# An encoder layer in split single precision: low parts by GpSimd instead of accumulating DMAs, and a convolution that accumulates in PSUM

## The chip, the core and the metric

The kernel runs on one core of a Trainium2 chip. The metric is the device time of one execution in microseconds (us). Before the change it is 1473.66 us, the median of 3 runs (1470.12 to 1475.76). The core has a matrix engine (TensorE, PE in the profile; its weight loads are PEld), three engines for elementwise work (VectorE, DVE; ScalarE, ACT; GpSimd, POOL), a queue that issues DMAs (SyncE, SP), and 16 DMA engines. GpSimd has a DMA queue of its own. Each engine works through its own instructions in the order of the program.

## What is computed

One layer is applied to two groups of tokens with the same weights: the prompt (512 tokens) and the sample (1024 tokens), both of width 1024. Everything is float32. Cut to what matters, and without biases:

```python
h = rms_norm(x, g_pre) * (1 + scale) + shift          # scale, shift, gate from c
a_val, a_glu, a_z, u, v, b_z, g_a, g_b = split(h @ w_in)   # 8 blocks of 1024 columns
a = depthwise_conv(a_val * sigmoid(a_glu), conv_w)    # 31 taps along the tokens
y_a = (silu(layer_norm(a)) * silu(a_z)) @ conv_proj
v = layer_norm(gelu(v))
mixed = einsum("gpq,bnqgc->bnpgc", w_s, v)            # chunks of 128 tokens
y_b = (gelu(u) * mixed * silu(b_z)) @ sgu_proj
m = sigmoid(g_a) * y_a + sigmoid(g_b) * y_b
out = x + gate * rms_norm(m @ w_out, g_post)
```

## The kernel before

**Split operands.** A float32 matrix is multiplied as a high part and a low part. `hi` is the matrix rounded to a shorter type (a cast on ACT) and `lo = x - hi`. A product is three matmuls: hi·hi, hi·lo and lo·hi (lines 449 to 451 for a block of output columns, 472 to 474 for a block of output rows, 483 to 485 for the sample's products). Almost all matmuls have 128 rows of weights and 512 columns.

**Units.** A unit is one 128x1024 block of weights (512 KB). SP loads it into a `raw` tile, ACT casts it to `hi` (line 247), and then the low part is made in one of two ways. With `by_dma`, ACT writes the rounded `-raw` into `lo` (line 250) and GpSimd's queue issues a DMA that adds `raw` to it (line 240), which leaves `raw - hi`. Without it, DVE subtracts (line 259). `raw`, `hi` and `lo` are rings of four tiles each, so a later load waits for the low part of an earlier unit.

**Order.** A planner in Python runs four clocks (PE, DVE, ACT and the plan of loads) while it writes the program. The list `steps` holds what PE does: a step of 24 matmuls is planned at 5.25 us (`PLAIN`), a product of 12 matmuls at half of that (`PROD`). Between the steps the planner puts the work that belongs to a step (`a1`, `d1`, `a2`, `d2`) and fills DVE's clock up with background generators (`bg`): the convolutions (`conv_gen`), the layer norms (`ln_gen`), the preparation of the sample's operands (`prep1` to `prep3`), and so on. So the order on every engine is fixed when the program is built.

**The stages on PE.** A head of some 45 us (modulation and the first seven column blocks in quarters). Then the prompt: the GLU columns (steps up to 16), the `v` columns (`steps_v`), `u`, `b_z` with the mixing products (`mix_mm`), the gates, the projections and `steps_o`. Then the `v` columns of the sample's halves `sa` and `sb`. Then 28 **pairs**: a pair takes two blocks of 128 columns and both halves of the sample through 7 products instead of 8. For this it needs sums and differences of the two weight blocks (`T12`, `T34`, lines 1056 to 1063, on DVE), which are split too: `a` is the block itself (DVE subtracts, line 1079), `b`, `c` and `d` are made by `neg` on ACT (line 1068) and the accumulating DMA. The pairs come in groups: 8 for the GLU, then gB, um (`u` times the mixed `v`), hB (times silu of `b_z`), z, gA, four pairs each. Last come the projections of the halves (`post_B`, `post_A`) and their outputs (`steps_o`).

**Results of a pair.** ACT snapshots the bank X or Z after a product (`snap`, line 1014), because the next product adds to the same bank. DVE then adds (`d_c11`, `d_c22`, `d_c12`, lines 1018 to 1026), ACT applies a function (lines 1126, 1148, 1167), and in um and hB DVE multiplies four times (line 1158). PSUM's eight banks form one ring of eight (`bank()`).

**The convolution.** 31 scalar_tensor_tensor instructions per channel block (line 403), two blocks in turn, each on 512 tokens (prompt) or 1024 (sample). The accumulator is in SBUF: in the slot `S` for the prompt, in `c` for the sample. The sample's results go to DRAM and come back for the layer norm (`late_ln`), whose two means are matmuls with a constant (`bcast_mean`, lines 331 and 332); in the program these stand in the steps of `post_B` and later.

## Time and profile before

The profiled execution took 1466.83 us; its trace spans 1464.9 us. The other runs took 1470.12 to 1475.76 us.

| | busy us | share of the span |
|---|---|---|
| PE | 1432.5 | 98% |
| DVE | 1129.0 | 77% |
| ACT | 742.3 | 51% |
| POOL | 186.2 | 13% |

The page's rows on DMA say that 229.85 MB go through SP's queue and 90.72 MB through GpSimd's; the chain of work that ended last is PE for 80% and DMA for 11%. A busy PE is not PE at its peak, since matmuls are pipelined and their ends are modelled; what is counted below is how many matmuls a stretch holds. In a row of the windows view the columns are the stretch, its length, then PE, PEld, DVE, ACT and POOL, each with busy us and (x instructions), then the granted TensorE clock, the busy share of the DMA engines, and GB/s.

### The profile page before, as it was taken

The page shows a single profiled execution, that of the slowest core. Times are in us where ns is not written, and L with a number is a line of the kernel's source. Part 1 is how long each engine was busy: PE and PEld are TensorE (multiplying, and loading weights), DVE is VectorE, ACT ScalarE, POOL GpSimd, SP SyncE. Part 2 cuts the span into 40 slices and gives each one's busy share as a digit, 9 for nine tenths or more (in the row PEclk, how much of TensorE's full clock was granted, in tenths as well). Part 3 has the DMA queues.
Part 4 walks back from the last instruction along what each step waited for, and adds up shares of the span by engine and source line. Part 5 has one row for each costly group of instructions (what it writes and reads, how often), then busy time and mean ns, then how long its engine had stood idle before and what let it go on. Part 6 is the DMA issues. An engine that isn't in the chain of part 4 may idle for free.

```text
span 1464.9 us, 17769 instructions
## 1 busy us (share of the span) xinstructions
PE 1432.5 (98%) x6332; PEld 1169.3 (80%) x6332; DVE 1129.0 (77%) x1596; ACT 742.3 (51%) x1064; POOL 186.2 (13%) x220
## 2 busy tenths in 40 slices
PE   8999999999999989999999999999999989999997
PEld 4688888888888878888888888877888867888886
DVE  6769999976356455867999898898999939587645
ACT  3532544553486454454545565555556545554442
POOL 0000111111111110011111111111111100000000
PEclk9999999999999999999999999999999999999999
DMA  9266787897999998967666878877977799878782
GB/s 342 79 215 182 198 201 166 203 256 181 279 266 244 284 263 272 281 168 201 155 158 166 209 194 242 255 211 218 256 192 191 194 307 276 265 222 237 211 269 72
DMA packets 120040, 321.68 MB, mean 220 GB/s; under 512 B 13328, under 2 KB 17040, under 8 KB 119184
## 3 DMA queue, kind: packets, MB, share of 16 engines
q1 hardware_dynamic: 88992, 229.85, 45.2%
q0 software_dynamic: 30960, 90.72, 33.7%
q8 instruction: 49, 0.80, 0.2%
q14 instruction: 39, 0.32, 0.1%
HBM read 182.10 MB, written 47.71 MB: 157 GB/s over the span
## 4 chain that ended last, share of the span: by engine, by line
PE 80%; DMA 11%; DVE 4%; issue 2%; ACT 2%; SPq 1%; DVEq 0%; ACTq 0%; POOLq 0%
PE b L451 11%; PE b L449 11%; PE b L450 11%; PE b L483 10%; PE b L484 10%; PE b L485 10%; PE b L473 4%; PE b L474 4%; PE b L472 4%; DMA lo<-raw 2%; DMA wk<-d 2%; PE b L568 1%; DMA raw<-in_w_blk_dram 1%; DMA raw<-in_sproj_dram 1%; DVE c L403 1%
## 5 line engine op out<-in xcount | busy, mean ns | idle before, releaser
L483 PE MATMUL b<-A,hi 128*128 128x512 f32 x784 | 306.8, 391 | 6.9 <-ACT wk L1014 6.9
L484 PE MATMUL b<-A,hi 128*128 128x512 f32 x784 | 305.8, 390 | 0.0
L485 PE MATMUL b<-A,lo 128*128 128x512 f32 x784 | 305.7, 390 | 0.0
L449 PE MATMUL b<-A,hi 128*128 128x512 f32 x776 | 303.7, 391 | 0.0
L451 PE MATMUL b<-A,lo 128*128 128x512 f32 x776 | 302.8, 390 | 0.2 <-DMA lo<-raw 0.2
L450 PE MATMUL b<-A,hi 128*128 128x512 f32 x776 | 302.8, 390 | 0.0
L403 DVE SCALAR_TENSOR_TENSOR c<-c,prm 128x1024 f32<-128x1024 f32 x240 | 297.3, 1278 | 0.6
L247 ACT CAST hi<-raw 128x1024 fp32r<-128x1024 f32 x145 | 152.0, 1048 | 262.4 <-DMA raw<-in_w_v_dram 61.7
L240 POOL DMA_DIRECT2D lo<-raw x131 | 113.4, 865 | 788.8 <-ACT lo L250 690.8
L483 PEld LDWEIGHTS b<-A,hi 128*128 128x128 f32 x784 | 147.6, 188 | 40.1 <-ACT wk L1014 9.7
L485 PEld LDWEIGHTS b<-A,lo 128*128 128x128 f32 x784 | 147.6, 188 | 30.5
L484 PEld LDWEIGHTS b<-A,hi 128*128 128x128 f32 x784 | 147.5, 188 | 30.6 <-DVE A L967 0.2
L451 PEld LDWEIGHTS b<-A,lo 128*128 128x128 f32 x776 | 146.1, 188 | 31.3 <-DMA lo<-raw 0.7
L449 PEld LDWEIGHTS b<-A,hi 128*128 128x128 f32 x776 | 146.1, 188 | 30.4 <-issue 0.2
L450 PEld LDWEIGHTS b<-A,hi 128*128 128x128 f32 x776 | 146.0, 188 | 30.5 <-issue 0.2
L403 DVE SCALAR_TENSOR_TENSOR S<-c,prm,S 128x512 f32<-128x512 f32 x240 | 162.6, 745 | 0.2
L473 PE MATMUL b<-lo,A 128*128 128x512 f32 x384 | 150.6, 392 | 5.0 <-DMA lo<-raw 5.0
L472 PE MATMUL b<-hi,A 128*128 128x512 f32 x384 | 150.8, 393 | 0.0
L474 PE MATMUL b<-hi,A 128*128 128x512 f32 x384 | 150.0, 391 | 0.0
L240 POOL DMA_DIRECT2D lo<-T x84 | 72.4, 862 | 456.7 <-ACT lo L1068 374.0
L1014 ACT COPY wk<-b 128x512 f32<-128x512 f32 x112 | 65.0, 585 | 121.2 <-PE b L485 117.5
L250 ACT ACTIVATE lo<-raw 128x1024 fp32r<-128x1024 f32 x103 | 108.7, 1055 | 0.0
(206 smaller groups left out, 1630.7 us busy)
## 6 DMA issues: line engine op xcount, KB each, us to landing
raw<-in_w_blk_dram SPq DMA_DIRECT2D x105, 512.0 KB, 5.6
lo<-raw POOLq DMA_DIRECT2D x103, 512.0 KB, 6.6
d<-wk SPq DMA_DIRECT2D x142, 256.0 KB, 3.7
wk<-d SPq DMA_DIRECT2D x116, 256.0 KB, 5.9
lo<-T POOLq DMA_DIRECT2D x28, 512.0 KB, 5.7
lo<-T POOLq DMA_DIRECT2D x56, 256.0 KB, 4.4
raw<-in_w_v_dram SPq DMA_DIRECT2D x24, 512.0 KB, 5.6
raw<-in_sproj_dram SPq DMA_DIRECT2D x24, 512.0 KB, 6.1
```

The source lines that it names most:

```text
L240: GP.dma_start(lo.bitcast(F32), src, accum_op=ALU.add)
L247: S.copy(u.hi, u.raw)
L403: lambda: V.scalar_tensor_tensor(acc, in0=win, scalar=wt, in1=acc, op0=ALU.mult, op1=ALU.add))
L449: PE.matmul(dst, lhsT=wh3[:, k, :], rhs=hi, start=(k == 0), stop=False)
L450: PE.matmul(dst, lhsT=wh3[:, k, :], rhs=lo, start=False, stop=False)
L451: PE.matmul(dst, lhsT=wl3[:, k, :], rhs=hi, start=False, stop=(k == NK - 1))
L472: PE.matmul(banks[i], lhsT=hi, rhs=wh3[:, kk, :], start=(k == 0), stop=False)
L473: PE.matmul(banks[i], lhsT=hi, rhs=wl3[:, kk, :], start=False, stop=False)
L474: PE.matmul(banks[i], lhsT=lo, rhs=wh3[:, kk, :], start=False, stop=(k == NK - 1))
L483: PE.matmul(dst, lhsT=wh3[:, k, :], rhs=hi, start=st, stop=False, skip_group_check=True)
L484: PE.matmul(dst, lhsT=wh3[:, k, :], rhs=lo, start=False, stop=False, skip_group_check=True)
L485: PE.matmul(dst, lhsT=wl3[:, k, :], rhs=hi, start=False, stop=sp, skip_group_check=True)
```

## The change

1. **Low parts.** Every low part of a unit and of a pair is a subtraction on GpSimd (`rest`, line 249 of the new file): `by_dma`, the negated copy on ACT, the accumulating DMA and DVE's subtractions (lines 259 and 1079) are gone. The head's first seven blocks keep DVE's.
2. **Sums of weights.** `T12` and `T34` are made by GpSimd (`gsub`), ahead of the low parts in the same queue.
3. **PSUM.** The ring of eight banks becomes a ring of four banks (`ps`) and two double banks (`pd`). The convolution's accumulators are double banks; so are the banks of the means, of the sample's mixing, and of the second half of `steps_v` (sample) and `steps_o`. At the end of a channel block ACT copies the accumulator out.
4. **Order.** The group gB moves behind z. The two layer norms of the sample follow the convolution directly and are written to DRAM as `hA`; the operands of `post_A` are then made like those of `post_B` (`act_gen`). A third window tile lets a convolution's input be fetched earlier.

The diff, cut to its core:

```diff
-    ps = ctx.enter_context(tc.tile_pool(name="ps", bufs=8, space=bass.MemoryType.PSUM))
+    ps = ctx.enter_context(tc.tile_pool(name="ps", bufs=4, space=bass.MemoryType.PSUM))
+    pd = ctx.enter_context(tc.tile_pool(name="pd", bufs=2, space=bass.MemoryType.PSUM))
...
+    def double():
+        return pd.tile([P, 2 * T], F32, tag="b2", name="b2")
+    def four(more):
+        if not more:
+            return [bank() for _ in range(4)]
+        d = [double(), double()]
+        return [d[i // 2][:, (i % 2) * T:(i % 2) * T + T] for i in range(4)]
...
-    def lo_by_dma(lo, src):
-        GP.dma_start(lo.bitcast(F32), src, accum_op=ALU.add)
+    def rest(lo, x, hi):
+        GP.tensor_tensor(out=lo, in0=x, in1=hi.bitcast(F32), op=ALU.subtract)
...
             S.copy(u.hi, u.raw)
             clk["act"] += 0.96
-            if u.by_dma:
-                S.activation(u.lo, u.raw, AF.Copy, scale=-1.0)
-                clk["act"] += 0.96
-                lo_by_dma(u.lo, u.raw)
-                u.raw = True
-                live["raw"] -= 1
-    def unit_dve(u):
-        if not u.by_dma and u.raw is not True:
-            r, h, w = u.raw, u.hi, u.lo
-            dv(1.14, lambda: V.tensor_sub(w, r, h.bitcast(F32)))
+            rest(u.lo, u.raw, u.hi)
             u.raw = True
             live["raw"] -= 1
...
-            b = bank()
+            b = double()[:, 0:T]
             PE.matmul(b, lhsT=onemr, rhs=hi, start=True, stop=False)
...
-                ch.acc = accs(ch.j)
+                ch.acc = double()[:, 0:w]
...
-                        banks[:] = [bank() for _ in range(4)]
+                        banks[:] = four(h == 1 and t is not t0)
...
-        m = bank()
+        m = bank() if t is t0 else double()[:, 0:T]
...
+        def gsub(o, x, y):
+            GP.tensor_tensor(out=o, in0=x, in1=y, op=ALU.subtract)
         def t12():
-            dv(0.65, lambda: V.tensor_sub(half(t_, 1), half(u2.raw, 0), half(u1.raw, 0)))
-            dv(0.65, lambda: V.tensor_sub(half(t_, 0), half(u2.raw, 1), half(t_, 1)))
+            gsub(half(t_, 1), half(u2.raw, 0), half(u1.raw, 0))
+            gsub(half(t_, 0), half(u2.raw, 1), half(t_, 1))
...
+        def both(n, x):
+            hi, lo = part_tile("hi"), part_tile("lo")
+            w[n] = (hi, lo)
+            S.copy(hi, x)
+            rest(lo, x, hi)
+            clk["act"] += 0.96
         def act_b():
-            neg(lo, w["t12"])
-            lo_by_dma(lo, w["t12"])
-            S.copy(hi, w["t12"])
-            clk["act"] += 1.92
+            both("b", w["t12"])
...
         def out(j, acc):
             accd[j] = scratch(D)
-            put(accd[j], acc)
-            free[j % 2] = clk["dve"] + 4.0
+            for i in range(2):
+                x = wk()
+                ac(0.53, lambda: S.copy(x, acc[:, i * T:(i + 1) * T]))
+                put(accd[j][:, i * T:(i + 1) * T], x)
...
-        yield from late_ln(sa)
+        for t in halves:
+            yield from late_ln(t)
...
             dv(0.62, lambda: V.tensor_mul(z, z, t.acc[j]))
-            kept[j] = (z, ac(0.53, lambda: S.copy(t.hA.hi(j), z)))
+            spill("hA", t.half, j, z)
...
-    for name, b0, fin in (("gB", 56, lambda j: pair_func("gB", AF.Sigmoid, j)),
-                          ("um", 24, lambda j: pair_mul("um", AF.Gelu_apprx_tanh, "mx", j)),
+    for name, b0, fin in (("um", 24, lambda j: pair_mul("um", AF.Gelu_apprx_tanh, "mx", j)),
                           ("hB", 40, lambda j: pair_mul("hB", AF.Silu, "um", j)),
                           ("z", 16, lambda j: pair_func("z", AF.Silu, j)),
+                          ("gB", 56, lambda j: pair_func("gB", AF.Sigmoid, j)),
```

GpSimd's queue in the pairs, before. A row is one instruction: its line, its kind, the tile that it writes, the tiles that it reads, and the shape. The rows are those of one pair (`lo` of b, of c in two halves, of d) and the first two of the next:

```order
L240 DMA lo_7781<-T12_7741 128x1024
L240 DMA lo_7828<-T34_7786 128x512
L240 DMA lo_7828<-raw_7639 128x512
L240 DMA lo_7878<-T34_7786 128x512
L240 DMA lo_7944<-T12_7904 128x1024
L240 DMA lo_7991<-T34_7949 128x512
```

The same place in the changed kernel, one pair:

```order
L1054 TENSOR_TENSOR T12_7384<-raw_7289,raw_7287 128x512
L1054 TENSOR_TENSOR T12_7384<-raw_7289,T12_7384 128x512
L249 TENSOR_TENSOR lo_7388<-raw_7287,hi_7387 128x1024
L1054 TENSOR_TENSOR T34_7430<-raw_7289 128x512
L1054 TENSOR_TENSOR T34_7430<-raw_7287,T12_7384 128x512
L249 TENSOR_TENSOR lo_7434<-T12_7384,hi_7433 128x1024
L249 TENSOR_TENSOR lo_7487<-T34_7430,hi_7486 128x512
L249 TENSOR_TENSOR lo_7487<-raw_7289,hi_7486 128x512
L249 TENSOR_TENSOR lo_7535<-T34_7430,hi_7534 128x512
```

Four DMA issues per pair have become nine subtractions, two of 1024 columns and seven of 512, all with operands in SBUF.

DVE in a pair of the group hB, before: the sums, the low part of a, the additions (lines 1018, 1022, 1026) and multiplications (line 1158) of the results, and the convolution (line 403, accumulator in the tile `c8`) between them:

```order
L1018 TENSOR_TENSOR wk_7875<-b_7883,wk_7875 128x512
L1056 TENSOR_TENSOR T12_7904<-raw_7803,raw_7801 128x512
L1057 TENSOR_TENSOR T12_7904<-raw_7803,T12_7904 128x512
L1079 TENSOR_TENSOR lo_7900<-raw_7801,hi_7899 128x1024
L1158 TENSOR_TENSOR wk_7875<-wk_7875,wk_7896 128x512
L403 SCALAR_TENSOR_TENSOR c8_5283<-c8_5283,prm_83 128x1024 x2
L1062 TENSOR_TENSOR T34_7949<-raw_7803 128x512
L1063 TENSOR_TENSOR T34_7949<-raw_7801,T12_7904 128x512
L403 SCALAR_TENSOR_TENSOR c8_5283<-c8_5283,prm_83 128x1024
L1022 TENSOR_TENSOR wk_7973<-wk_7973,wk_7941 128x512
```

In the changed kernel, the first half of a pair of the same group (line 1019 was 1018, 1023 was 1022, 1151 was 1158, 402 was 403):

```order
L1019 TENSOR_TENSOR wk_7198<-b_7205,wk_7198 128x512
L402 SCALAR_TENSOR_TENSOR b2_6938<-c8_5158,prm_86,b2_6938 128x1024
L402 SCALAR_TENSOR_TENSOR b2_6582<-c8_5158,prm_86,b2_6582 128x1024
L1151 TENSOR_TENSOR wk_7198<-wk_7198,wk_7218 128x512
L402 SCALAR_TENSOR_TENSOR b2_6938<-c8_5158,prm_86,b2_6938 128x1024
L402 SCALAR_TENSOR_TENSOR b2_6582<-c8_5158,prm_86,b2_6582 128x1024
L402 SCALAR_TENSOR_TENSOR b2_6938<-c8_5158,prm_86,b2_6938 128x1024
L402 SCALAR_TENSOR_TENSOR b2_6582<-c8_5158,prm_86,b2_6582 128x1024
L1023 TENSOR_TENSOR wk_7297<-wk_7297,wk_7265 128x512
```

The five instructions on weights are gone and taps of the convolution stand in their place, with the accumulator in the double banks `b2`.

PE at the first mean of the sample's layer norm, before: the mean (lines 331 and 332) stands within a step of `post_B` (lines 449 to 451):

```order
L449 MATMUL b_9609<-A_9313,hi_9454 128x512
L450 MATMUL b_9609<-A_9313,hi_9454 128x512
L451 MATMUL b_9609<-A_9313,lo_9455 128x512
L331 MATMUL b_9622<-wk_9546,onemr_90 128x512
L332 MATMUL b_9622<-wk_9547,onemr_90 128x512
L449 MATMUL b_9609<-A_9314,hi_9454 128x512
```

and in the changed kernel between two products of a pair (lines 482 to 484):

```order
L482 MATMUL b_8486<-A_3844,hi_8341 128x512
L483 MATMUL b_8486<-A_3844,hi_8341 128x512
L484 MATMUL b_8486<-A_3844,lo_8342 128x512
L330 MATMUL b2_8499<-wk_8476,onemr_93 128x512
L331 MATMUL b2_8499<-wk_8477,onemr_93 128x512
L482 MATMUL b_8461<-A_4307,hi_8390 128x512
```

All four means of the sample's layer norms now stand in the last seven pairs; before, two stood in `post_B` and two in `post_A` and the output of the first half.

## The prediction

> **What bounds the kernel now.** First the page's busy times, then the work of each engine in stretches of 50 us, because a share over the whole span hides the stalls.

> ```profile
> PE 1432.5 (98%) x6332; PEld 1169.3 (80%) x6332; DVE 1129.0 (77%) x1596; ACT 742.3 (51%) x1064; POOL 186.2 (13%) x220
> ```
> ```profile
> 0.00:50.00 50.00, 42.59 (x151) 24.02 (x152) 33.97 (x58) 22.18 (x32) 0.49 (x5) 0.93 0.87 308
> ...
> 500.00:550.00 50.00, 45.42 (x191) 36.43 (x190) 25.12 (x41) 24.44 (x38) 5.16 (x6) 0.97 0.96 270
> ...
> 800.00:850.00 50.00, 49.62 (x219) 40.78 (x218) 44.74 (x48) 26.74 (x41) 7.76 (x9) 1.00 0.75 198
> ...
> 900.00:950.00 50.00, 49.40 (x218) 40.62 (x217) 44.19 (x52) 27.23 (x44) 8.94 (x11) 1.00 0.90 258
> 950.00:1000.00 50.00, 48.57 (x214) 39.68 (x214) 44.94 (x51) 27.50 (x44) 8.35 (x10) 1.00 0.83 231
> 1000.00:1050.00 50.00, 48.20 (x213) 39.59 (x212) 45.81 (x52) 27.73 (x45) 9.48 (x11) 1.00 0.81 220
> 1050.00:1100.00 50.00, 49.43 (x219) 40.58 (x217) 46.66 (x49) 27.17 (x43) 7.75 (x9) 1.00 0.81 217
> ...
> 1150.00:1200.00 50.00, 47.87 (x205) 39.14 (x204) 28.18 (x32) 23.11 (x38) 5.16 (x6) 0.97 0.85 248
> 1200.00:1250.00 50.00, 45.48 (x190) 36.31 (x189) 43.42 (x67) 28.55 (x37) 4.44 (x5) 0.97 0.95 306
> 1250.00:1300.00 50.00, 50.00 (x222) 41.34 (x222) 30.70 (x45) 24.98 (x32) 3.44 (x4) 1.00 0.83 249
> ...
> 1450.00:1465.00 15.00, 6.60 (x30) 5.12 (x28) 10.40 (x41) 1.38 (x4) 0.00 (x0) 0.82 0.34 126
> ```

> An undisturbed stretch holds 222 matmuls of 512 columns, so one takes 50/222 = 0.225 us. The stretches with fewer are the stalls: 31 missing at 500, 3 at 800, 4 at 900, 8 at 950, 9 at 1000, 3 at 1050, 17 at 1150 and 32 at 1200. That is 107 matmuls or 24.1 us. The head (151) and the tail (30 matmuls in 15 us) are outside the change. Since no matmul is added or removed beside means that only move, **24.1 us is nearly all that can be won**: the profiled 1466.83 us could become 1442.7. Next, who ends those stalls:

> ```profile
> PE b L483 <- ACT wk L1014: 6.9, 6, 2.1
> PE b L473 <- DMA lo<-raw: 5.0, 4, 2.6
> PE b L331 <- ACT wk L320: 4.1, 2, 2.6
> ```
> ```profile
> 520.45 0.50 PE L473 MATMUL b<-lo,A 128*128 128x512 f32 x1 [2.61 <-DMA lo<-raw]
> ...
> 521.40 0.63 PE L473 MATMUL b<-lo,A 128*128 128x512 f32 x1
> 521.83 0.63 PE L474 MATMUL b<-hi,A 128*128 128x512 f32 x1
> ```

> These waits are 16 us; the rest of the 24.1 is the clock behind them. After the pause of 2.61 us the matmuls start 0.43 us apart instead of 0.225 (the granted clock of that stretch is 0.97 against 1.00), so a long stall costs more than itself. Behind the waits stand loads and the DMAs that make low parts:

> ```profile
> lo<-raw POOLq DMA_DIRECT2D x103, 512.0 KB, 6.6
> ```
> ```profile
> q0 software_dynamic: 30960, 90.72, 33.7%
> ```
> ```profile
> 1200.92 1.22 DVE L259 TENSOR_TENSOR lo<-raw,hi 128x1024 fp32r<-128x1024 f32 x1 [15.26 <-ACT hi L247]
> ```
> ```profile
> 1163.60 8.39 DMA raw<-in_sproj_dram
> ```

> A low part by DMA takes a median 6.6 us to land, and GpSimd's queue takes 33.7% of the DMA engines. At 1201 DVE had stood 15.26 us before the low part of a weight block whose load was late, and the layer norm (L331) queued behind it on DVE. The 1163.60 row is a piece of the chain that ended last.

> **The change part by part: what goes.** The prices:

> ```profile
> L403 DVE SCALAR_TENSOR_TENSOR c<-c,prm 128x1024 f32<-128x1024 f32 x240 | 297.3, 1278 | 0.6
> L259 DVE TENSOR_TENSOR lo<-raw,hi 128x1024 fp32r<-128x1024 f32 x42 | 51.3, 1221 | 41.8 <-ACT hi L247 41.3
> L1079 DVE TENSOR_TENSOR lo<-raw,hi 128x1024 fp32r<-128x1024 f32 x28 | 34.1, 1218 | 0.0
> ...
> L1022 DVE TENSOR_TENSOR wk<-wk 128x512 f32<-128x512 f32 x28 | 19.2, 687 | 15.8 <-ACT wk L1014 15.7
> L1018 DVE TENSOR_TENSOR wk<-b,wk 128x512 f32<-128x512 f32 x28 | 19.2, 684 | 1.8 <-PE b L485 1.3 <-issue 0.4 <-ACT A L1269 0.2
> ```
> ```profile
> L250 ACT ACTIVATE lo<-raw 128x1024 fp32r<-128x1024 f32 x103 | 108.7, 1055 | 0.0
> ```
> ```profile
> L240 POOL DMA_DIRECT2D lo<-raw x131 | 113.4, 865 | 788.8 <-ACT lo L250 690.8 <-DVE S L403 18.3 <-DMA raw<-in_cproj_dram 14.5
> ...
> L192 POOL TENSOR_SCALAR_AFFINE_SELECT ident<-ones 128x128 f32<-128x128 f32 x1 | 0.3, 287 | 0.6 <-DVE ones L188 0.6
> ```

> ACT loses 108.7 us of negated copies (and line 1068's), DVE 51.3 + 34.1 us of low parts and the sums of weights. None of this shortens the path by itself: PE paces every stage. What counts is that a low part no longer crosses the DMA engines, that DVE no longer waits for a load in order, and that `raw` comes free sooner, so loads start earlier on queues with a third less traffic. All 24.1 us hang on such latencies, and I take them as gone: 1442.7 us. The means at 1200 and 1228 leave the projections for the pairs.

> **What is added on GpSimd.** No row shows a GpSimd subtraction. From below it is DVE's 1.22 us (L259); from above, the only GpSimd arithmetic there is, L192 with 287 ns for 128 columns, gives 2.3 us for 1024. I take 2.3, the same engine's row, and 1.15 for 512. A pair then holds 2 x 2.3 + 7 x 1.15 = 12.65 us, against 84 matmuls x 0.225 = 18.9 us on PE: GpSimd is busy 0.67 of the pair, in the column steps 2.3 of 5.4 us. A ring tile is free five products (13.5 us) before its use, so cast (as line 250's 1.055 us) and subtraction, 1.05 + 2.3 us, fit with some 10 us to spare. GpSimd is not the bound.

> **DVE beside GpSimd.** Both read SBUF at once, and no row of before shows that: its GpSimd rows are DMA issues. A DVE instruction with two tensors in SBUF could wait for a GpSimd instruction in flight. The wait w per such instruction is nothing from below; a gain is excluded, since no engine is sped up by it. If each waits for the GpSimd instruction to end, a pair gives 0.67 x 0.78 = 0.52 us (0.78 is the mean remainder, (4.6 x 1.15 + 8.05 x 0.575)/12.65), and 0.78 if GpSimd is always found busy. No row is nearer to either end; I take 0.26, half of 0.52, and keep 0 to 0.78. [...]

> The taps have one input in PSUM now and are not counted. That PSUM costs DVE nothing I take from L1018, which reads a bank, against L1022, which doesn't: 684 and 687 ns. Writing a bank has no row. From below a tap stays at 1278 ns; from above it doubles the fixed 0.2 us of L403 (1278 ns less 1024 columns at 1.04 ns), which would put 12 x 0.2 = 2.4 us on a pair; I take 0, the nearest row. [...]

> What slack does DVE have? Its order is filled to the planner's clock, 7 x 2.625 = 18.375 us a pair, and its real starts run a little ahead of that:

> ```profile
> 859.45 0.68 DVE L1018 TENSOR_TENSOR wk<-b,wk 128x512 f32<-128x512 f32 x1
> ...
> 878.07 0.68 DVE L1018 TENSOR_TENSOR wk<-b,wk 128x512 f32<-128x512 f32 x1
> ...
> 886.06 0.69 DVE L1022 TENSOR_TENSOR wk<-wk 128x512 f32<-128x512 f32 x1 [0.65 <-ACT wk L1014]
> ...
> 896.72 0.69 DVE L1018 TENSOR_TENSOR wk<-b,wk 128x512 f32<-128x512 f32 x1
> ```

> One pair takes DVE 18.62 us, the next 18.65 with idle time in it, so 0.3 to 1.3 us below PE's 18.9; I use 1.0. Behind a late DVE stand ACT's functions, and behind these its snapshots, which PE needs:

> ```profile
> L1014 ACT COPY wk<-b 128x512 f32<-128x512 f32 x112 | 65.0, 585 | 121.2 <-PE b L485 117.5 <-DMA d<-wk 3.7
> L1126 ACT ACTIVATE wk<-wk 128x512 f32<-128x512 f32 x36 | 22.7, 631 | 41.5 <-DVE wk L1022 20.9 <-DVE wk L1018 19.8 <-DVE wk L1026 0.8
> ```

> Counted from the end of product Y, the sum ends at about 1.3 (two of 0.65), its function at 1.95, the snapshot takes 0.585 and must be over two products (5.4 us) after Y, so **2.8 us of lag are free** and all beyond stalls PE. Now the new stalls, at w = 0.26 (w = 0, 0.52 in brackets):

> ```profile
> 223.03 1.05 PE L568 MATMUL b<-wsT_t,S 128*128 128x128 f32 x8
> ```
> ```profile
> 230.41 0.74 DVE L573 SCALAR_TENSOR_TENSOR wk<-b,prm,bias_t 128x512 f32<-128x512 f32 x1
> ```
> ```profile
> 151.18 0.39 PE L474 MATMUL b<-hi,A 128*128 128x512 f32 x1
> ...
> 152.75 2.07 ACT L541 ACTIVATE S<-b 128x512 f32<-128x512 f32 x4
> ```

> - `v` of the prompt: its two halves use the same four banks, and ACT's reads began at 152.75 where PE's first half ended with the matmul of 151.18, so the second could start at some 151.3. With a cast less ahead of them 1.5 us stay (1.5; 1.5).
> - `b_z` of the prompt: a mixing bank written at 223.03 is read until 231.15; in a ring of four it is needed again two steps on, at 235.7, so 4.6 us are free. Three contended instructions a step, eight steps, DVE full: 0.21 x 3 x 8 = 5.0, less 4.6 = 0.4 (0; 5.4, with 0.42 from 2.3 of 6.35 us busy).
> - The sample's sums: 28 contended instructions, partly paid by eight L259 that leave: 2 (0; 4).
> - GLU pairs: the last bank is needed one product later and read by DVE until 2.0 us, 0.7 to spare: 1 (0; 2).
> - um and hB: five contended instructions against 1.0 us: 0.3 x 8 = 2.4 is below 2.8, but the multiplications come in clusters: 2 (0; 1.6 x 8 - 2.8 = 10).
> - Means in the pairs: PE waits for DVE's lag at four of them: 3 (2; 4).
> - Projections: 1.5 (0.5; 2).

> Sum 11.4 us: 1442.7 + 11.4 = 1454.1 in the profiled execution. The median of the runs lies 6.8 us above it (1473.66 against 1466.83), and I carry that over: **1461 us**.

> **The rivals.**
> 1. *No contention* (w = 0). New stalls 4 us, so 1446.7, as a median 1453.5. For it: the taps, DVE's largest group, leave the shared reads. Against: five instructions a pair still have both inputs in SBUF.
> 2. *A full wait* (w = 0.52): 28.9 us of new stalls, 1471.6, as a median 1478: what goes comes back. [...]
> 3. *The lag becomes the bound, slower.* If each of these instructions meets a busy GpSimd (w = 0.78), um and hB cost 2.9 x 8 - 2.8 = 20 us, GLU 5, `b_z` and the sums 6 each, the means 6, the rest 4: about 48, so 1491, as a median 1497. It needs 0.7 of GpSimd's time to become nearly all, which waiting on both sides can do. Slower by over 0.5% begins near w = 0.6.
> 4. *The change doesn't do what it says*: stalls come from loads that are as late as before (the 8.39 us row). Half of the 24 stays: 1466, as a median about 1470.
> 5. *GpSimd is the bound*: over 3.4 ns a column a pair exceeds PE's 18.9 us; at 4.5, twice L192's, 28 x 6.4 = 180 us more.

> **How the numbers follow.** Chances: forecast 0.30, first rival 0.22, second 0.20, third 0.15, fourth 0.08, fifth 0.05. Half a per cent, 7.4 us, is about what a measurement can tell. Faster (below 1466.3): the first, nearly all of the forecast, a little of the fourth, 0.51; slower (above 1481): third and fifth and a fifth of the second, 0.24; the rest 0.25. The range reaches from the first rival, with 3 us for a better head, to near the third: 1450 to 1494. Cases of both signs hold most of the chance; the forecast's own range is 1453 to 1468.

> **What would show it.** Right: no L473 wait on a DMA, full stretches of 222 up to 600, L1018's successors of 0.69 us, GpSimd rows of 2.3 us. Contention shows as DVE instructions with two SBUF inputs longer than 0.69 us while taps stay at 1.28, and as snapshots late in um and hB. Taps above 1.28 us would make PSUM the cause. GpSimd rows above 3.4 us would make the whole sum wrong.

## The result and the profile after

The changed kernel takes 1527.93 us (median of 4 runs, 1525.07 to 1530.42) against 1471.89 us: **slower by 3.8%** (ratio 1.0383, interval 1.0342 to 1.0424). The forecast was 1461 us with a range of 1450 to 1494.

First the same two views as before: the page's busy times, and the work in stretches (columns as explained with the profile before).

```profile
PE 1456.5 (95%) x6332; PEld 1182.4 (77%) x6332; DVE 1186.9 (78%) x1416; ACT 598.7 (39%) x881; POOL 764.1 (50%) x402
```
```profile
300.00:350.00 50.00, 45.39 (x188) 36.66 (x187) 45.52 (x54) 18.08 (x25) 22.11 (x9) 0.93 0.40 137
350.00:400.00 50.00, 41.08 (x168) 32.80 (x168) 34.22 (x44) 11.24 (x15) 17.35 (x6) 0.93 0.27 101
...
450.00:500.00 50.00, 46.31 (x192) 37.47 (x191) 41.51 (x44) 22.22 (x33) 19.89 (x8) 0.93 0.33 106
...
600.00:650.00 50.00, 40.73 (x180) 33.24 (x179) 31.85 (x48) 14.94 (x21) 17.21 (x7) 0.86 0.49 170
650.00:700.00 50.00, 44.62 (x198) 36.53 (x197) 34.83 (x45) 16.11 (x25) 27.82 (x16) 0.93 0.34 117
...
1150.00:1200.00 50.00, 43.76 (x178) 35.22 (x177) 33.08 (x30) 33.09 (x44) 34.22 (x20) 0.93 0.53 177
```

GpSimd is busy half the span, the DMA engines 0.27 to 0.53 of these stretches where it was 0.71 to 0.97. The five stretches shown from 300 to 700 us held 219 to 254 matmuls before and now hold 168 to 198. DVE is not full in the six: 32 to 46 of 50 us.

For all kernels below, stalls are counted from the trace as the distance between the starts of two matmuls where it is over 0.3 us, less 0.227 us, the commonest distance in both traces. "Tail" is what lies between the last matmul's end and the end of the span.

| us | before the pairs (from 45 us) | in the pairs | behind them | tail | median |
|---|---|---|---|---|---|
| before | 10.8 | 10.7 | 7.2 | 8.3 | 1471.9 |
| after | 50.3 | 26.4 | 7.4 | 12.8 | 1527.9 |

The profiled spans differ by 63.7 us (1528.6 and 1464.9). Stalls and tail hold 60 of it, two thirds in the stages ahead of the pairs. The waits of PE in the new profile (total us, times, longest):

```profile
PE b L330 <- ACT wk L319: 11.6, 2, 7.0
PE b L482 <- ACT wk L1015: 11.6, 7, 4.4
PE b L567 <- DVE c L556: 11.4, 3, 6.7
PE b L450 <- POOL lo L249: 4.9, 4, 1.9
```

The waits on `lo<-raw` by DMA are gone. What PE waits for now is mostly ACT and DVE: means of the prompt's layer norm (L330, at 313 and 365 us), snapshots (L482), the layer norm of `v` ahead of the mixing (L567). The groups of DVE and of GpSimd say why:

```profile
L402 DVE SCALAR_TENSOR_TENSOR b<-c,prm,b 128x1024 f32<-128x1024 f32 x240 | 295.1, 1280 | 0.6
...
L517 DVE TENSOR_TENSOR A<-wk,A 128x512 fp32r<-128x512 f32 x40 | 52.7, 1318 | 19.6 <-ACT A L514 19.5
L1151 DVE TENSOR_TENSOR wk<-wk 128x512 f32<-128x512 f32 x32 | 36.4, 1157 | 0.8 <-ACT wk L1141 0.8
L580 DVE TENSOR_TENSOR wk<-wk,S 128x512 f32<-128x512 f32 x24 | 35.8, 1491 | 0.8
...
L1023 DVE TENSOR_TENSOR wk<-wk 128x512 f32<-128x512 f32 x28 | 32.5, 1162 | 18.5 <-ACT wk L1015 18.4
...
L1019 DVE TENSOR_TENSOR wk<-b,wk 128x512 f32<-128x512 f32 x28 | 19.1, 684 | 5.1 <-issue 3.4 <-ACT wk L1015 1.7
```
```profile
L249 POOL TENSOR_TENSOR lo<-raw,hi 128x1024 fp32r<-128x1024 f32 x173 | 431.6, 2499 | 562.5 <-ACT hi L256 550.3 <-PE b L472 6.1 <-ACT hi L1075 3.4
L1054 POOL TENSOR_TENSOR T<-raw 128x512 f32<-128x512 f32 x56 | 77.5, 1385 | 0.0
```

Instructions of 512 columns with both operands in SBUF (L517, L580, L1151, L1023) went from 0.69 us to a mean of 1.16 to 1.49; L1019, which reads one from a PSUM bank, stayed at 0.684, and the taps with their accumulator in PSUM at 1.28. Over all groups, 148 DVE instructions ran more than 0.1 us longer than the shortest of their group, and lost 202 us together. A few of them have one tensor, read from and written to SBUF: L556, the tensor_scalar that L567 waits for, took up to 2.83 us instead of 0.81. The timeline of one stall shows the mechanism. Its columns are start, duration, engine, line, and in brackets the idle time before and what ended it:

```profile
464.02 2.72 POOL L249 TENSOR_TENSOR lo<-raw,hi 128x1024 fp32r<-128x1024 f32 x1 [1.29 <-ACT hi L256]
464.41 2.88 DVE L769 TENSOR_TENSOR wk<-wk,S 128x512 f32<-128x512 f32 x1
467.33 0.62 ACT L514 CAST A<-wk 128x512 fp32r<-128x512 f32 x1 [3.38 <-DVE wk L769]
...
470.09 1.03 ACT L256 CAST hi<-raw 128x1024 fp32r<-128x1024 f32 x1
471.02 0.62 ACT L514 CAST A<-wk 128x512 fp32r<-128x512 f32 x1
471.20 2.53 POOL L249 TENSOR_TENSOR lo<-raw,hi 128x1024 fp32r<-128x1024 f32 x1 [4.45 <-ACT hi L256]
471.67 2.60 DVE L517 TENSOR_TENSOR A<-wk,A 128x512 fp32r<-128x512 f32 x1 [0.16 <-ACT A L514]
...
474.32 0.79 PE L449 MATMUL b<-A,hi 128*128 128x512 f32 x1 [2.13 <-DVE A L517]
...
475.34 0.63 PE L448 MATMUL b<-A,hi 128*128 128x512 f32 x1
475.77 0.63 PE L449 MATMUL b<-A,hi 128*128 128x512 f32 x1
```

DVE's L769 begins 0.39 us after GpSimd's subtraction and ends 0.55 us after that one's end (466.74). It has stood until GpSimd was through and then taken about its usual time (L769 before: 0.69 us). So it is with nearly all: 144 of the 148 end within 0.2 us of the time that comes out when their usual time is added to the end of a subtraction. The next hold is no accident: ACT's queue holds the cast of a unit (L256), which starts GpSimd, and right behind it the cast of an operand (L514), which starts DVE's L517 half a microsecond later. PE waits for that L517, and after the pause its matmuls start 0.43 us apart.

The tail has another cause. Of the last output's four row blocks, each two share a double bank now. ACT's squares (L609) of blocks two to four, with PE's last matmul, after:

```profile
1508.37 0.60 ACT L609 ACTIVATE wk<-b 128x512 f32<-128x512 f32 x1
...
1515.39 0.39 PE L473 MATMUL b<-hi,A 128*128 128x512 f32 x1
...
1515.87 0.60 ACT L609 ACTIVATE wk<-b 128x512 f32<-128x512 f32 x1 [6.81 <-PE b L473]
...
1516.59 0.60 ACT L609 ACTIVATE wk<-b 128x512 f32<-128x512 f32 x1
```

and of blocks three and four before:

```profile
1452.62 0.60 ACT L610 ACTIVATE wk<-b 128x512 f32<-128x512 f32 x1 [3.39 <-PE b L474]
...
1456.69 0.60 ACT L610 ACTIVATE wk<-b 128x512 f32<-128x512 f32 x1 [3.39 <-PE b L474]
```

The third block's square used to start 4.1 us before the fourth's; now it starts after the last matmul, and the whole chain of both blocks lies behind PE's end.

### The profile page after: what moved, and what is told of

It reads as the page before. It is cut to its first block, busy times and chain, and to the rows that moved or that the text cites. A ratio compares the mean times of both kernels' runs of the same rounds, so it can differ in the third digit from the quotient of the medians.

```text
span 1528.6 us, 17582 instructions
## 1 busy us (share of the span) xinstructions
PE 1456.5 (95%) x6332; PEld 1182.4 (77%) x6332; DVE 1186.9 (78%) x1416; ACT 598.7 (39%) x881; POOL 764.1 (50%) x402
## 4 chain that ended last, share of the span: by engine, by line
PE 42%; DVE 39%; DMA 7%; issue 5%; ACT 4%; SPq 1%; POOL 1%; DVEq 0%; ACTq 0%
DVE b L402 17%; PE b L482 7%; PE b L484 6%; PE b L483 6%; PE b L471 3%; PE b L472 3%; PE b L473 3%; PE b L450 3%; PE b L449 2%; PE b L448 2%; DMA wk<-d 2%; DMA raw<-in_w_blk_dram 2%; DVE wk L1151 2%; DVE wk L580 1%; DVE A L517 1%
## 5 line engine op out<-in xcount | busy, mean ns | idle before, releaser
L249 POOL TENSOR_TENSOR lo<-raw,hi 128x1024 fp32r<-128x1024 f32 (+1 forms) x201 | 472.3, 2353 | 562.5 <-ACT hi L256 550.3
L402 DVE SCALAR_TENSOR_TENSOR b<-c,prm,b 128x512 f32<-128x512 f32 (+1 forms) x480 | 456.9, 1017 | 1.0
L482 PE MATMUL b<-A,hi 128*128 128x512 f32 x784 | 308.9, 394 | 11.7 <-ACT wk L1015 11.6
L483 PE MATMUL b<-A,hi 128*128 128x512 f32 x784 | 307.4, 392 | 0.0
L256 ACT CAST hi<-raw 128x1024 fp32r<-128x1024 f32 x145 | 151.9, 1048 | 269.1 <-DMA raw<-in_w_v_dram 58.9
L249 POOL TENSOR_TENSOR lo<-T,hi 128x512 fp32r<-128x512 f32 (+1 forms) x84 | 144.5, 1720 | 168.4 <-ACT hi L1099 87.4
L482 PEld LDWEIGHTS b<-A,hi 128*128 128x128 f32 x784 | 148.5, 189 | 46.0 <-ACT wk L1015 15.1
L449 PEld LDWEIGHTS b<-A,hi 128*128 128x128 f32 x776 | 147.8, 190 | 33.7 <-DVE A L517 2.4
L483 PEld LDWEIGHTS b<-A,hi 128*128 128x128 f32 x784 | 148.6, 190 | 30.7
L471 PE MATMUL b<-hi,A 128*128 128x512 f32 x384 | 152.7, 398 | 4.1 <-DVE wk L579 3.7
L473 PE MATMUL b<-hi,A 128*128 128x512 f32 x384 | 151.3, 394 | 0.0
L471 PEld LDWEIGHTS b<-hi,A 128*128 128x128 f32 x384 | 73.4, 191 | 21.1 <-DVE wk L579 4.8
L472 PEld LDWEIGHTS b<-lo,A 128*128 128x128 f32 x384 | 73.5, 191 | 17.4 <-POOL lo L249 2.2
## 6 DMA issues: line engine op xcount, KB each, us to landing
raw<-in_w_blk_dram SPq DMA_DIRECT2D x105, 512.0 KB, 4.9
raw<-in_w_v_dram SPq DMA_DIRECT2D x24, 512.0 KB, 4.5
raw<-in_sproj_dram SPq DMA_DIRECT2D x24, 512.0 KB, 4.6
raw<-in_cproj_dram SPq DMA_DIRECT2D x24, 512.0 KB, 3.7
raw<-in_w_out_dram SPq DMA_DIRECT2D x24, 512.0 KB, 4.1
S<-in_w_ada_dram SPq DMA_DIRECT2D x16, 512.0 KB, 7.0
```

What stands on the lines that cost most here:

```text
L249: GP.tensor_tensor(out=lo, in0=x, in1=hi.bitcast(F32), op=ALU.subtract)
L256: S.copy(u.hi, u.raw)
L402: lambda: V.scalar_tensor_tensor(acc, in0=win, scalar=wt, in1=acc, op0=ALU.mult, op1=ALU.add))
L449: PE.matmul(dst, lhsT=wh3[:, k, :], rhs=lo, start=False, stop=False)
L471: PE.matmul(banks[i], lhsT=hi, rhs=wh3[:, kk, :], start=(k == 0), stop=False)
L472: PE.matmul(banks[i], lhsT=hi, rhs=wl3[:, kk, :], start=False, stop=False)
```

## The experiments

The theory: (1) a DVE instruction with two operands in SBUF stands until the GpSimd subtraction in flight has ended, and these holds make the stalls. Rivals: (2) the rings of four and two and the new order make them; (3) GpSimd's writes hold DVE too; (4) loads are late in any case; (5) GpSimd's low parts are merely late. All ratios are against the kernel before, on the same chip. The expectations speak of 57 us of stalls before the pairs and 20 in them, where the table has 50.3 and 26.4: split at 700 and 1200 us instead of at the pairs' first and last matmul, the same stalls give 56.8 and 19.1.

**GpSimd busy, but not reading.** First a short memset, then one as long as the subtraction; the order is unchanged.

```diff
     def rest(lo, x, hi):
-        GP.tensor_tensor(out=lo, in0=x, in1=hi.bitcast(F32), op=ALU.subtract)
+        GP.tensor_tensor(out=lo[:, 0:8], in0=x[:, 0:8], in1=hi[:, 0:8].bitcast(F32), op=ALU.subtract)
+        GP.memset(lo[:, 8:].bitcast(F32), 0.001)
```

with the same edit in `gsub`; the second run issues each memset twice, with 192 columns more where the tile is long.

> Every GpSimd subtraction of the changed kernel becomes a subtraction of 8 columns and a memset of the rest, in the same place of the same order; the low parts and sums of weights are then not the real ones. Theory 1 (a DVE instruction with two operands in SBUF stands until the GpSimd subtraction in flight has ended; 202 us of DVE are lost so): DVE rows of two SBUF operands return to 0.68 to 0.75 us, the stalls before the pairs shrink from 57 to some 15 us, the median is 1455 to 1475. Theory 2 (the rings of four banks and two double banks, and the later start of the prompt's convolution, cause the loss): the order is the same, so the median stays above 1510. Theory 3 (a write by GpSimd holds DVE up too): rows over 1 us stay, 1490 to 1525.

> As the run with 8 columns and a memset, but the memset is issued twice and a piece more, so that GpSimd is busy about 2.4 us for 1024 columns and 1.3 us for 512, as long as its subtractions; the low parts are again not the real ones. Theory 1 (GpSimd's reads hold DVE up): still 1447 to 1457. Theory 5 (the low parts of the changed kernel come late because GpSimd takes 2.4 us, and the shorter memset cured that): back to 1490 to 1528.

Measured: 1448.6 us (ratio 0.9855, 0.9829 to 0.9882), below its range, and 1450.8 us (0.9871, 0.9846 to 0.9895), within it. Both kernels leave the true low parts out, so they only measure. In the second run stalls are 5.7 before the pairs, 1.7 in them and 0 behind. Its groups of DVE (the last an instruction with one tensor), and of GpSimd:

```profile
L521 DVE TENSOR_TENSOR A<-wk,A 128x512 fp32r<-128x512 f32 x40 | 27.5, 688 | 20.8 <-ACT A L518 20.8
...
L1027 DVE TENSOR_TENSOR wk<-wk 128x512 f32<-128x512 f32 x28 | 19.3, 690 | 27.2 <-ACT wk L1019 27.2
...
L560 DVE TENSOR_SCALAR c<-c,mv,r 128x1024 f32<-128x1024 f32 x8 | 7.3, 979 | 0.1
```
```profile
L251 POOL MEMSET lo<- 128x1016 f32 x201 | 191.8, 954 | 11.6
L250 POOL MEMSET lo<- 128x1016 f32 x201 | 190.3, 947 | 0.0
L249 POOL TENSOR_TENSOR lo<-raw,hi 128x8 fp32r<-128x8 f32 x201 | 61.1, 304 | 502.7 <-ACT hi L260 501.9 <-ACT hi L1081 0.7
```

GpSimd is busy for 712 us in this run against 764, and a low part is complete as late as with a subtraction, yet DVE's two-operand rows (L521 and L1027 are L517 and L1023 of the changed kernel) are back at 0.69. So rival 5 falls, and rival 3 for instructions with two operands. Writes do hold some with one: in this run 21 DVE instructions, all tensor_scalar or copy, ran more than 0.1 us longer than the shortest of their group and lost 11 us, up to 0.86 us each, nearly all until a memset had ended (L560, the L556 of the changed kernel, has a mean of 0.98 us instead of 0.81). Rival 4 falls too, since the same loads leave 7.4 us of stalls in all, and rival 2 for the kernel as it stands: the same order and rings, without the reads, are faster than the kernel before. **GpSimd's reading of SBUF costs 1527.9 - 1450.8 = 77 us**, and the stalls alone differ by as much.

**Which reads.** Units or pairs, or both, get their low parts in the old way:

```diff
             S.copy(u.hi, u.raw)
             clk["act"] += 0.96
-            rest(u.lo, u.raw, u.hi)
+            S.activation(u.lo, u.raw, AF.Copy, scale=-1.0)
+            clk["act"] += 0.96
+            GP.dma_start(u.lo.bitcast(F32), u.raw, accum_op=ALU.add)
```

That is the first run, all units by DMA. The second restores the old mix of the units, the third undoes the pairs' part (`t12`, `t34` and `dve_a` on DVE, `neg` and the DMA for b, c and d), the fourth both:

```diff
+            if u.by == "dve":
+                return
...
+    def unit_dve(u):
+        if u.by == "dve" and u.raw is not True:
+            dv(1.14, lambda: V.tensor_sub(w, r, h.bitcast(F32)))
```
```diff
-            gsub(half(t_, 1), half(u2.raw, 0), half(u1.raw, 0))
+            dv(0.65, lambda: V.tensor_sub(half(t_, 1), half(u2.raw, 0), half(u1.raw, 0)))
...
-            rest(lo, x, hi)
+            neg(lo, w["t12"])
+            lo_by_dma(lo, w["t12"])
```

> The low parts of the units go back to the negated copy on ACT and the accumulating DMA; the pairs keep GpSimd. Theory 1: outside the pairs no DVE row is longer than its base, of the 57 us of stalls before the pairs some 40 go, 9 us in the pairs stay: median 1480 to 1492. Theory 2: no change, 1520 to 1532. Theory 4 (a DMA's low part is as late as GpSimd's, because the loads are what is late): 1505 to 1525.

> The units' low parts exactly as in the kernel before (by the accumulating DMA or by DVE, after the old rule; not all by DMA as in the run of 1526 us, whose stalls wait for DMA lo<-raw), the pairs by GpSimd. Theory 1: stalls before the pairs fall from 57 to 10 to 15 us, 18 in the pairs and 7 behind them stay, 4.5 us stay in the tail: median 1478 to 1492. Theory 2 (rings and order): 1515 and more.

> The pairs' sums of weights go back to DVE and their low parts to DVE and the accumulating DMA, as before the change; the units keep GpSimd. Theory 1: only the 20 us of stalls inside the pairs can shrink, to the 11 of the kernel before: median 1515 to 1525. Theory 2 (the order): 1523 to 1532, with the same stalls in um and hB.

> All low parts and sums of weights as in the kernel before, with the rings, the convolution in PSUM and the order of the changed kernel; GpSimd subtracts nothing. Theory 1: no DVE row is longer than its base; stalls before the pairs 10, in the pairs 10, and behind them what the layer norms' backlog on DVE costs without contention, 10 to 30; tail 4.5: median 1472 to 1500. Theory 2: over 1510, with stalls where the changed kernel has them.

Measured (the stalls as above):

| low parts | median, ratio (interval) | before the pairs | in them | behind |
|---|---|---|---|---|
| units and pairs by GpSimd (the change) | 1527.9, 1.038 (1.034 to 1.042) | 50.3 | 26.4 | 7.4 |
| units all by DMA | 1525.8, 1.037 (1.032 to 1.041) | 34.2 | 23.6 | 20.2 |
| units in the old mix | 1498.3, 1.019 (1.017 to 1.021) | 23.6 | 26.7 | 4.0 |
| pairs in the old way | 1546.1, 1.051 (1.048 to 1.055) | 49.9 | 9.4 | 42.8 |
| both in the old way | 1506.7, 1.025 (1.022 to 1.027) | 22.6 | 9.0 | 29.1 |

All four lie outside the time that theory 1 gave, and the first lies where theory 2 had it (1520 to 1532), though each stage moves as theory 1 says: the holds go where the reads go (none are left with both undone), the pairs' stalls fall from 26 to 9, those ahead of the pairs from 50 to 23. What theory 1 left out: with all units by DMA the waits change their owner (26.6 us on `lo<-raw` by DMA). In the old mix 12 us of that stay:

```profile
PE b L489 <- DMA lo<-raw: 7.7, 6, 3.0
...
PE b L467 <- DMA lo<-raw: 4.4, 3, 2.2
```

And without GpSimd in the pairs DVE is late for the layer norms and the operands of the projections, which the new order packs behind the convolution. PE's waits with both undone, where nothing is held any more:

```profile
PE b L468 <- ACT A L1278: 15.2, 3, 6.4
PE b L492 <- DMA lo<-raw: 8.9, 3, 3.6
```

So part 4 of the change needs the DVE time that GpSimd frees in the pairs: with the pairs' subtractions on GpSimd, the stalls behind them fall from 29.1 to 4.0 us. The units' low parts on GpSimd cost 30 to 39 us against the old mix (1527.9 against 1498.3, 1546.1 against 1506.7), the pairs' on GpSimd gain 8 to 18. One part of rival 2 stands: with the old low parts and nothing held, the new rings, accumulators and order are 2.5% slower than the kernel before. Why low parts by DMA come later here than in the kernel before, ahead of the pairs, stays open.

**The length of a hold.** Each subtraction in pieces of 256 columns:

```diff
+    def sub(o, x, y):
+        for i in range(0, o.shape[-1], 256):
+            GP.tensor_tensor(out=o[:, i:i + 256], in0=x[:, i:i + 256], in1=y[:, i:i + 256], op=ALU.subtract)
```

> Every GpSimd subtraction is cut into pieces of 256 columns (estimated 0.19 + 256 x 2.15 ns = 0.74 us each, by the 1.29 and 2.39 us of 512 and 1024). Theory 1 with the wait ending at the instruction in flight: the longest wait of one DVE instruction falls from 2.2 to about 0.75 us, the DVE time lost from 202 to 90 to 130 us, the median to 1485 to 1510. If GpSimd holds DVE until its queue is empty, the waits stay at 2 us and more and the median at 1528 or above.

Measured: 1487.4 us (1.0121, 1.0092 to 1.0150). DVE loses 133 us instead of 202, a little over the 90 to 130 expected; the stalls fall from 50 to 24 us ahead of the pairs and from 26 to 17 in them. Its DVE groups and its largest GpSimd group:

```profile
L521 DVE TENSOR_TENSOR A<-wk,A 128x512 fp32r<-128x512 f32 x40 | 38.7, 968 | 19.3 <-ACT A L518 19.2
...
L1027 DVE TENSOR_TENSOR wk<-wk 128x512 f32<-128x512 f32 x28 | 33.5, 1195 | 17.3 <-ACT wk L1019 17.3
```
```profile
L250 POOL TENSOR_TENSOR lo<-raw,hi 128x256 fp32r<-128x256 f32 x748 | 635.4, 882 | 392.1 <-ACT hi L260 388.4 <-ACT hi L1079 3.6
```

The longest of the 40 L521 falls from 2.65 to 1.24 us. So a hold mostly ends with the instruction in flight and not with GpSimd's queue, though GpSimd is busy longer (975 us against 764): 271 of the 278 held instructions lost no more than 0.75 us, one piece. The other seven stood through two to four pieces in a row and lost up to 2.72 us, which was not expected; what decides between the two is not shown. Five of the seven are L1027, which gains nothing (1195 against 1162 ns). Eight of L1660 in a row, from 327.96 us on, took 1.22 us each instead of 0.74.

**The taps.** The convolution's accumulators go back to SBUF, two windows instead of three in the sample's:

```diff
-                ch.acc = double()[:, 0:w]
+                ch.acc = accs(ch.j)
...
+        accs = [c[:, 2 * W2 + i * D:2 * W2 + (i + 1) * D] for i in range(2)]
```

> The changed kernel with the convolution's accumulators back in SBUF, so that its 480 taps have two operands in SBUF. Theory 1: taps grow longer than 1.28 us beside GpSimd; if the two exclude each other fully, a pair with the convolution needs 13.7 us of taps, 1.5 of other two-operand work, 13.8 of GpSimd and 1.5 us of the rest, 30.5 against 18.9 us, and a step of the prompt 2.4 us more: 1600 to 1850. If taps are not held up: 1520 to 1545, and the PSUM accumulators were of no use.

Measured: 1768.4 us (1.2022, 1.1983 to 1.2062; two runs). The taps, GpSimd's sums, and what PE waits for:

```profile
L402 DVE SCALAR_TENSOR_TENSOR c<-c,prm 128x1024 f32<-128x1024 f32 x240 | 461.3, 1963 | 1.0
```
```profile
L1054 POOL TENSOR_TENSOR T<-raw 128x512 f32<-128x512 f32 x56 | 110.0, 1965 | 0.0
```
```profile
PE b L482 <- ACT wk L1015: 143.7, 25, 11.4
```

With two operands in SBUF the taps are held as well (1963 ns where they took 1280 in the changed kernel), and GpSimd's sums are longer beside them (1965 ns instead of 1385). The pairs' stalls are 200 us, where full exclusion was reckoned at 244 (some 21 pairs with the convolution, 11.6 us more in each). Without the accumulators in PSUM the change would have lost 297 us instead of 56.

**Versions.** Units in the old mix ahead of the pairs, pieces of 256 columns from there on, and the tail's edit; then the tail's edit alone on top of the pieces; then both with the old mix in two stretches only.

```diff
-                        banks[:] = four(h == 1)
+                        banks[:] = four(h == 1) if not (final and h == 1) else [
+                            double()[:, 0:T], double()[:, 0:T], bank(), bank()]
```

> A version that should beat both: units as before the change ahead of the pairs, GpSimd's subtractions in pieces of 256 columns from the pairs on, and the last output's four row blocks in four PSUM tiles of their own (in the changed kernel two blocks share a double bank, and ACT's square of the third block waits for the last matmul of the fourth: the span ends 12.8 us after the last matmul instead of 8.3). Theory 1: stalls of 10 before the pairs, 10 in them and about none behind, against 28.6 before the change: median 1458 to 1470.

> As the run in pieces of 256 columns (1487.4 us), with one edit: the last output's four row blocks lie in four PSUM tiles instead of two double banks. If two blocks that share a tile make ACT wait for the later block's matmuls, the span ends 8.3 us behind the last matmul instead of 12.8 and the median is 1481 to 1484; if the tail has another cause, it stays at 12.8 and 1487.

> As the run in pieces of 256 columns with the tail's edit, and the units of two stretches (steps 46 to 60 and 94 to 103, where the layer norms of the prompt and of the sample's v stall PE by 11 and 17 us) get their low parts as before the change, by the accumulating DMA or by DVE. Theory 1: those stalls fall to some 4 and 4 us: median 1459 to 1470. If DVE's backlog there has other causes (DVE's own subtractions, late loads): 1475 to 1485.

The first took 1479.1 us (1.0074, 1.0047 to 1.0101) and missed: 28.8 us of stalls ahead of the pairs, 13.5 of the waits on `lo<-raw` by DMA. The second took 1482.2 us (1.0077, 1.0054 to 1.0100), as expected, against 1487.4 without the edit, with a tail of 8.0 us; its squares of the third and fourth block start 4.1 us apart again, so the shared tile was the cause:

```profile
1468.69 0.60 ACT L614 ACTIVATE wk<-b 128x512 f32<-128x512 f32 x1 [3.39 <-PE b L477]
...
1472.77 0.60 ACT L614 ACTIVATE wk<-b 128x512 f32<-128x512 f32 x1 [3.39 <-PE b L477]
```

The third took **1465.6 us**, ratio 0.9973 (0.9950 to 0.9995), again as expected: a gain of 0.3% over the kernel before, the best of three versions, which the interval just sets apart from nothing. Its stalls are 7.8 before the pairs, 18.3 in them and 0.3 behind. The units of steps 46 to 60 and 94 to 103, made in the old way, took 16.7 of the 24.5 us of stalls ahead of the pairs away.

## Why the prediction was wrong

**What held.** With the reads gone, stalls of 28.7 us (10.8, 10.7 and 7.2) shrink to 7.4, so the 24 us that the prediction took as gone were nearly all to be had. A subtraction on GpSimd takes 2.50 us and 1.39 us (L249, L1054; means, holds included) where 2.3 and 1.15 were taken, and GpSimd, busy for 764 of 1528.6 us, is not the bound. Taps in PSUM cost next to nothing: for 1024 columns 1280 ns against 1278 before, with a start-to-start distance of two taps in a row of 1.192 us against 1.196, and for 512 columns 754 ns against 745. Only the tensor_scalar that begins a channel block became longer, from 810 to 1342 ns for 1024 columns and from 540 to 811 for 512, eight of each.

**The wait itself was somewhat too small.** Taken was w = 0.26 for each instruction with two tensors in SBUF, and 0.52 by the second rival. In the changed kernel it is 0.30 before the pairs (82 us over 274 instructions), 0.45 in them (64 over 141) and 0.37 behind (47 over 128). Instructions with two inputs in SBUF stood until the subtraction ended (144 of the 148 above, the few with one tensor among them), and beside GpSimd's memsets they took 0.688 us (L521 of the run with long memsets). With one of the two inputs in PSUM they were not held (L1019, 0.684 us). The prediction counted only instructions with two tensors in SBUF; it left out the tensor_scalar and copy instructions, which were held too, even by memsets (L556 had a mean of 1.18 us in the changed kernel and 0.98 us beside the memsets, against 0.81).

**The step that failed is the list of new stalls.** Against the run with long memsets, the changed kernel has 44.6 us more ahead of the pairs, 24.7 in them and 7.4 behind. The list gave 3.9, 6 and 1.5 at w = 0.26, and 10.9, 16 and 2 even at a full wait. For the pairs at a full wait that is two thirds; ahead of them it is short by a factor of four. The prediction asked for DVE's slack in the pairs only and priced, elsewhere, three places: the banks of `v`, `b_z`, the sample's sums. The layer norms of the prompt, its gates and output, and the `v` of the sample, some 400 us, were given nothing. Yet the trace has 17.5 us of stalls at the prompt's layer norm (313 to 371 us), 13.0 between 471 and 528, and 14.6 between 622 and 655, up to the mixing of the sample's `v`. In the pairs, where the list had 2 us for um and hB (10 at a full wait), PE stalls 8.7 us from 894 to 1038; 6.6 us at the mixing of `v` (690 to 702) stand nowhere in it, and where it had 3 us for the means, these cost 1.1 us but snapshots beside the layer norms 9.9 (1169 to 1196). Ahead of the pairs DVE had stood idle for much of the time before the change:

```profile
300.00:350.00 50.00, 50.00 (x222) 41.32 (x221) 38.40 (x62) 26.70 (x34) 7.75 (x9) 1.00 0.91 232
350.00:400.00 50.00, 49.76 (x219) 40.69 (x218) 18.88 (x29) 20.86 (x26) 6.91 (x8) 1.00 0.89 235
```

The prediction gives no reason for the nothing; in effect it takes this idle time (12 and 31 us of 50) as cover.

It is no cover, for two reasons that the trace shows. A hold is not spread: 49 of the 274 instructions carry 81 of the 82 us, 1.7 us each, where a meeting at random with a subtraction of 2.4 us would cost half of it, 1.2. Half of the holds ahead of the pairs (27 of 52) begin 0.3 to 0.7 us after a subtraction's start; where the timeline above shows it, ACT's queue starts the one and then the other. And these instructions stand on a chain without slack: cast on ACT, subtraction on DVE, matmul on PE, next result, each waiting for the one before. The stalls of PE that come of the 82 us are more than half of them, 44.6, the slower matmuls after each pause included.

**One term was missing**, the double banks' tail, 4.5 us: the prediction looked at the banks as a ring and not at two results in one tile. The third rival, the one on the slower side, had its threshold at w = 0.6, with most of the price again placed in the pairs; the loss came at less.

So the second rival's mechanism is what happened, at a wait below its own, and its time of 1478 was still 50 us short: the sum was made mainly where DVE had looked full.

## What to carry to other kernels

Work for an idle GpSimd was not free here: its reads of SBUF cost 77 us. Count every DVE instruction with two SBUF operands in its neighbourhood, and ask of each whether PE is waiting behind it, whether or not DVE's share of the stretch is low. Put one operand in PSUM where that can be had (L1019 stayed at 0.684 us and the taps at 1.28, where L1023 went from 0.69 to 1.16), and cut GpSimd's instructions short, since most holds here lasted no longer than the one in flight (in pieces of 256 columns 271 of 278 lost at most 0.75 us, and the changed kernel became 40 us faster). A reader of one result in a shared PSUM tile waited here for the matmuls of the other as well, so the last ones of a kernel should have tiles of their own (the tail was 12.8 us with shared tiles and 8.0 without).

## What the runs showed of the hardware that was not expected

```profile
387.10 9.37 DVE L1656 SCALAR_TENSOR_TENSOR wk<-c,sc,wk 128x512 f32<-128x512 f32 x14
```
```profile
391.27 10.22 POOL L249 TENSOR_TENSOR lo<-raw,hi 128x1024 fp32r<-128x1024 f32 x2 [13.82 <-ACT hi L256]
```

Two subtractions took 10.22 us, 5.4 more than twice their usual 2.4: the first took 7.4 and ended at 398.68 us, 2.2 us after the end of the row (396.47). Very short instructions were held as well: a DVE one of 128x4 elements (L174, at 684.6 us of the changed kernel) took 2.3 us instead of 0.16.
